# The context stream's modulation products move from VectorE to GpSimd and ScalarE in a hybrid-backbone inference step

## The chip, the core and the metric

The kernel runs on one core of a Trainium2 chip. The metric is the device time of one launch in microseconds: 1493.95 us as the median of two runs (1492.44 and 1495.47). Engines are named as in the profile: PE is TensorE (PEld its weight loads), DVE VectorE, ACT ScalarE, POOL GpSimd, SP SyncE, which here issues all DMAs. Each engine carries out its instructions in the order in which they stand in its queue; a semaphore wait at the head holds up what is behind it.

## What is computed

One inference step of a two-layer backbone on 512 latent and 128 context tokens of 1024 features. Each layer has a mixer (attention and a spatial gating in layer 0, a short gated convolution in layer 1) and a squared-ReLU MLP with 4096 hidden features. Shift, scale and gate of each come from a modulation of the two conditioning vectors, one for the latent tokens and one for the context tokens:

```python
def adaln(cvec, w_mod, b_mod):
    m = jax.nn.silu(cvec) @ w_mod + b_mod
    return [t[:, None, :] for t in jnp.split(m, 6, axis=-1)]

sh_p, sc_p, ga_p, shf_p, scf_p, gaf_p = adaln(c_ctx[None, :], w_mod, b_mod)
sh_s, sc_s, ga_s, shf_s, scf_s, gaf_s = adaln(c, w_mod, b_mod)
hs = xs * (1.0 + sc_s) + sh_s
xs = layer_norm(ALPHA * xs + ga_s * out_s, g_mix, bt_mix)
fs = sq_relu_mlp(xs * (1.0 + scf_s) + shf_s, w_ff1, w_ff2)
xs = layer_norm(ALPHA * xs + gaf_s * fs, g_ff, bt_ff)
```

## The kernel before

Everything lies feature by token: a tile has 128 features on the partitions and 640 tokens on the free axis, in two halves of 320. A float32 product is three passes of the array over operands that are split into a high and a low part. ScalarE makes the high part (line 66 for weights, 241 for a block's input `hn`, 990 for hidden features `hid`), VectorE the low part (67, 242, 992).

The weights are a stream of 188 strips of 1024x128 (`strip`, `prepare`). A strip's float32 copy is loaded into `raw`, one of four buffers, and split into one of seven `w` tiles. A strip's product with one half is 24 matmuls into one PSUM bank, of which six are used in turn. Strips 28 to 35 are the first eight up strips of layer 0's MLP, 36 to 43 its first eight down strips; three more such groups of 16 follow. The first six up strips are gone through half by half, since the norm of the second half is still being formed then; the others strip by strip.

Most of the modulation is a product on TensorE. Seven sections are not: the MLP gate of layer 0 and all six of layer 1. `mod_products` forms them "in the background" while the MLP of layer 0 runs. A section has eight steps, one for 128 features. A step loads 128 rows of the transposed modulation weights into a buffer of the same four `raw` (line 175) and forms, for both streams, the sum over 1024 columns of the weights times the conditioning row `srows` (line 178: one VectorE instruction with two inputs, whose accumulator goes to `modT`). The instruction's other output is not used. `mods` sets the rates: the first section four steps for each strip that is fetched (two strips, 34 and 35), the other six sections one step for each strip.

A scheduler sets the order of each engine's queue from the program's order and its own estimate of the times, and gives out the four `raw` buffers. An instruction of a new kind can move its neighbours.

What the prediction also speaks of: line 240 forms a block's input from the normed residual on ScalarE; line 967 scales the residual there (16 passes, not urgent); lines 989 to 992 turn an up strip's PSUM into `hid` (relu and square on ScalarE, then two VectorE passes, the first with one input in PSUM); line 1038 is a GpSimd memset.

Of the kernel before, what the change touches and what calls it, by code (L numbers as in the profile page):

```python
"""One inference step of the hybrid backbone on one core.

Everything on the chip is kept feature-major ([feature on partitions, token on the free axis]),
512 latent tokens then 128 context tokens, so that products chain without transposes, the adaLN
terms are per-partition scalars and the depthwise convolution slides along the free axis.

Float32 products: each operand is split exactly into hi + lo of 12 significant bits (float32r), and
hi*hi + hi*lo + lo*hi are three passes of the array that accumulate in float32 in PSUM.
"""
# [16 lines left out]
P = 128  # L26
D = 1024
# [15 lines left out]
AHEAD = 36  # products of the out projection before the spatial gating, which they then alternate with  # L43
WARM = (10, 18, 12)
# The attention's pieces in the order in which they are issued. By two blocks of queries: a, b the
# softmax of each, V the values; by head: C, X the same for the context, N the norm's scales, M the
# norm; F half a strip of the projections.
# [5 lines left out]
def build(ctx, tc, io):  # L53
# [9 lines left out]
    # ---------------------------------------------------------------- helpers  # L63
    def split(hl, src):
        """hl[:, 0] = hi, hl[:, 1] = lo of src (a float32 tile in SBUF)."""
        S.copy(out=hl[:, 0], in_=src)  # L66
        V.tensor_tensor(out=hl[:, 1], in0=src, in1=hl[:, 0].bitcast(F32), op=ALU.subtract)  # L67
# [3 lines left out]
    def mm3(ps, lhs, rhs, first, last):  # L71
        """ps += lhs.T @ rhs; lhs(i), rhs(i) give part i (0 hi, 1 lo)."""
        for n, (i, j) in enumerate(PASSES):
            nc.tensor.matmul(ps, lhs(i), rhs(j), start=first and n == 0, stop=last and n == 2)  # L74

    # ------------------------------------------------- the stream of weights
# [21 lines left out]
    def strip(ahead=True, behind=None):  # L98
        """The next strip; loads those ahead, and a round of the background, behind the instruction given."""
# [8 lines left out]
    # -------------------------------------------------------------- constants  # L108
# [10 lines left out]
    def start_load(out, in_):  # L119
        """The loads that the start needs, in this order."""  # L120
# [13 lines left out]
    # ------------------------------------------------------------------ adaLN  # L134
# [5 lines left out]
    # [stream, section, tile]; sections: shift, scale + 1, gate, twice  # L140
# [9 lines left out]
    def mod_section(layer, sec, ps, rows):  # L150
        """A section of a layer's modulation for both streams: KT steps and a last one."""
# [19 lines left out]
    def mod_products(layer, sec, rows):  # L171
        """A section of a layer's modulation on VectorE, from the transposed weights: KT steps."""
        for f in range(KT):
            raw = raw_tile()
            nc.sync.dma_start(out=raw, in_=io["wmodT"][6 * layer + sec - 5, f])
            for i in range(2):
                out = raw if i == 1 else tp.tile([P, D], mybir.dt.bfloat16, name="unused", tag="acc", bufs=1)
                V.scalar_tensor_tensor(out=out, in0=raw, scalar=1.0, in1=rows[:, i], op0=ALU.mult, op1=ALU.mult,  # L178
                                       accum_out=modT[layer][:, i, sec, f:f + 1])
# [14 lines left out]
    def behind(gen, rate):  # L194
        """Run rate steps of gen with every strip that is fetched."""
        background.append([gen, rate])
# [20 lines left out]
    def mod_products_start(raws, ps):  # L217
        """A feature tile of layer 0's first shift and scale: four partial sums, for both streams."""
# [5 lines left out]
    def mod_finish_start(f, ps, rows):  # L224
        """Their sum, features on partitions."""
# [8 lines left out]
    # The input of a block: x * (1 + scale) + shift, split.  # L234
    def modulate(hl, x, sc, sh, segs, tmp_pool, c0):
        """hl[:, :, cols] from x (its columns start at c0); sc(i), sh(i): [P, 1] by stream."""
# [10 lines left out]
    # =================================================== phase 1: mixer of layer 0  # L247
# [15 lines left out]
    # The start: q and k of two heads, tile by tile as the modulation's weights arrive.  # L263
# [39 lines left out]
    with tc.manual_schedule(engines={mybir.EngineType.PE}):  # L303
        start_ps[3, 0] = mmp.tile([P, HALF], F32, name="mm")

        def keep_warm(n):
            """Products that nobody reads, while there are no others: the array's clock falls when it idles."""
# [41 lines left out]
    def proj_halves(w):  # L349
        """One 128-feature strip over all tokens: the two halves' PSUM tiles, in turn."""  # L350
# [14 lines left out]
    def rotary(kind, h, f):  # L365
        """The rotary on the latent columns, split."""
# [18 lines left out]
    def token_major(consume, tile_, between=None):  # L385
        """[128 tokens, 256 features] for the five token tiles, twice; strips: k quadruples."""
# [24 lines left out]
    def softmax_pair(q, k, qc, kc, nkeys):  # L411
        """(p1 - lam p2) * 2^-E for 128 queries (columns qc) over keys kc..kc+nkeys."""
# [34 lines left out]
    def values(h, pair, es):  # L447
        """The head's values for two blocks of queries."""
# [20 lines left out]
    def context_values(h, e):  # L469
        """The same for the context's queries, which attend to the context's keys alone."""  # L470
# [10 lines left out]
    def attention_scales(h):  # L481
        """RMS norm over the head's 128 features: each token's -2 / sqrt(mean square + EPS)."""
# [30 lines left out]
    def g_consume(t, block, ps):  # L513
        """Layer norm within each group, per token."""
# [38 lines left out]
    # lambda, and a power of two that keeps the attention's output in range  # L553
# [55 lines left out]
    def gates(tag, width):  # L609
        """Two of u's strips, kept in float32."""  # L610
# [7 lines left out]
    def fillers():  # L618
        """Products that run while a softmax does."""
# [601 lines left out]
```

## Time and profile before

| | |
|---|---|
| median of the runs | 1493.95 us (1492.44, 1495.47) |
| span of the profiled execution | 1490.6 us |
| PE busy | 1477.9 us (99%) |
| DVE busy | 894.6 us (60%) |
| ACT busy | 558.2 us (37%) |
| POOL busy | 2.2 us |
| DMA | 161.85 MB, mean 109 GB/s |

The span runs from the first to the last instruction of the profiled execution; that execution's own time is not listed beside it, so the runs' median stands for it. The busy time of an engine is the time in which at least one of its instructions ran; its idle time is put down to what released it. TensorE's granted clock is at its upper level, 2.4 GHz, in each stretch shown below (1.00 in the profile's rows).

### The profile page before, as it was taken

Reading aid. Unit: us, or ns where it says so; the run is one execution under the profiler, and the core shown is the slowest. Engines: PE = TensorE matmul, PEld = TensorE weight load, DVE = VectorE, ACT = ScalarE, POOL = GpSimd, SP = SyncE. Lnnn points to the kernel's source line nnn. Section 1 sums busy time; section 2 is a strip of 40 time slices with the busy share of each in tenths; the row PEclk is TensorE's granted clock in tenths of the full one; section 3 lists DMA queues with packets and bytes.
Section 4 is the critical chain, followed back from the end, with each engine's and each line's share of the span. In section 5 each row is a group of like instructions: output and inputs, shape, how many; then the busy total and the mean of one; then the engine's idle time right before and its main releaser. Section 6 shows DMA issues by size and latency. Waiting matters only on the chain.

```text
span 1490.6 us, 24292 instructions
## 1 busy us (share of the span) xinstructions
PE 1477.9 (99%) x10126; PEld 1426.1 (96%) x10126; DVE 894.6 (60%) x1726; ACT 558.2 (37%) x1032; POOL 2.2 (0%) x11
## 2 busy tenths in 40 slices
PE   8999999999999999999999999999999999999998
PEld 7779888999999999999999999999999999999997
DVE  3656855789986596586557534449533433433456
ACT  3435655346613213213317522216712312312313
POOL 0000000000000000000000000000000000000000
PEclk9999999999999999999999999999999999999999
DMA  9762015322664274275211322212222222222102
GB/s 353 197 206 78 31 36 199 112 88 71 211 227 142 85 226 142 78 222 154 86 54 59 102 83 71 80 35 86 86 85 73 83 71 71 85 72 71 58 1 71
DMA packets 50877, 161.85 MB, mean 109 GB/s; under 512 B 8400, under 2 KB 12112, under 8 KB 50640
## 3 DMA queue, kind: packets, MB, share of 16 engines
q1 hardware_dynamic: 50768, 160.31, 33.9%
q8 instruction: 79, 1.29, 0.4%
q14 instruction: 30, 0.25, 0.0%
HBM read 157.13 MB, written 3.15 MB: 108 GB/s over the span
## 4 chain that ended last, share of the span: by engine, by line
PE 95%; DVE 2%; DMA 1%; ACT 1%; issue 0%; SPq 0%; ACTq 0%; DVEq 0%
PE mm L74 86%; PE sc L425 2%; PE mod L157 1%; PE po L74 1%; PE mm L751 1%; DMA raw<-wmod 1%; PE pt L459 1%; PE ms L221 1%; PE mm L309 0%; PE st L940 0%; DVE w L67 0%; DMA mraw<-wstart 0%; PE ss L488 0%; PE rb L504 0%; PE st L927 0%
## 5 line engine op out<-in xcount | busy, mean ns | idle before, releaser
L74 PE MATMUL mm<-hn,w 128*128 128x320 f32 x4224 | 624.8, 310 | 0.5 <-ACT hn L241 0.5
L74 PEld LDWEIGHTS mm<-hn,w 128*128 128x128 f32 x4224 | 620.4, 188 | 2.9 <-ACT hn L241 1.7
L74 PE MATMUL mm<-hid,w 128*128 128x320 f32 x3072 | 453.4, 309 | 0.0
L74 PEld LDWEIGHTS mm<-hid,w 128*128 128x128 f32 x3072 | 451.2, 188 | 0.5
L66 ACT CAST w<-raw 128x1024 fp32r<-128x1024 f32 x188 | 196.6, 1047 | 368.6 <-PE mm L74 283.5
L67 DVE TENSOR_TENSOR w<-raw,w 128x1024 fp32r<-128x1024 f32 x188 | 229.4, 1222 | 172.2 <-ACT w L66 170.9
L677 DVE SCALAR_TENSOR_TENSOR xa<-mm,modT,xa 128x128 f32<-128x128 f32 (+2 forms) x264 | 108.0, 435 | 152.5 <-PE mm L74 152.4
L989 ACT ACTIVATE relu<-mm 128x320 f32<-128x320 f32 x128 | 55.7, 436 | 236.3 <-PE mm L74 236.3
L74 PE MATMUL mm<-hin,w 128*128 128x320 f32 x576 | 97.7, 315 | 0.3 <-DVE w L67 0.2
L991 DVE TENSOR_TENSOR relu<-relu,mm 128x320 f32<-128x320 f32 x128 | 61.5, 483 | 54.9 <-ACT hid L990 54.9
L74 PEld LDWEIGHTS mm<-hin,w 128*128 128x128 f32 x576 | 85.1, 188 | 6.1 <-issue 4.3
L178 DVE SCALAR_TENSOR_TENSOR unused<-raw,srows 128x1024 bf16<-128x1024 f32 x56 | 68.4, 1221 | 33.2 <-DMA raw<-wmodT 33.1
L74 PEld LDWEIGHTS mm<-w,hin 128*128 128x128 f32 x480 | 59.4, 190 | 16.7 <-issue 15.2
L178 DVE SCALAR_TENSOR_TENSOR raw<-raw,srows 128x1024 f32<-128x1024 f32 x56 | 68.2, 1219 | 0.5
L74 PE MATMUL mm<-w,hin 128*128 128x256 f32 x480 | 65.6, 288 | 0.4 <-DVE w L67 0.4
L992 DVE TENSOR_TENSOR hid<-relu,hid 128x320 fp32r<-128x320 f32 x128 | 62.5, 491 | 3.2
L990 ACT ACTIVATE hid<-relu 128x320 fp32r<-128x320 f32 x128 | 60.2, 472 | 2.0
L74 PE MATMUL mm<-mx,w 128*128 128x320 f32 x384 | 57.5, 310 | 0.0
L74 PEld LDWEIGHTS mm<-mx,w 128*128 128x128 f32 x384 | 56.5, 188 | 0.5 <-DVE mx L67 0.2
L74 PE MATMUL mm<-mix,w 128*128 128x320 f32 x288 | 43.2, 311 | 0.0
L74 PEld LDWEIGHTS mm<-mix,w 128*128 128x128 f32 x288 | 42.5, 188 | 0.3
L240 ACT ACTIVATE hf<-xa,np 128x192 f32<-128x192 f32 (+1 forms) x72 | 36.8, 560 | 4.5 <-DVE xa L944 4.2
(218 smaller groups left out, 937.0 us busy)
## 6 DMA issues: line engine op xcount, KB each, us to landing
raw<-wall SPq DMA_DIRECT2D x188, 512.0 KB, 3.6
raw<-wmodT SPq DMA_DIRECT2D x56, 512.0 KB, 3.7
raw<-wmod SPq DMA_DIRECT2D x24, 512.0 KB, 5.2
mraw<-wstart SPq DMA_DIRECT2D x16, 512.0 KB, 10.6
x<-xT SPq DMA_DIRECT2D x4, 640.0 KB, 10.0
xa<-xT SPq DMA_DIRECT2D x8, 320.0 KB, 4.5
yT<-xa SPq DMA_DIRECT2D x8, 320.0 KB, 2.3
srows<-silu_rows SPq DMA_DIRECT2D x1, 1024.0 KB
```

Of the source, the lines that this page charges most:

```text
L66: S.copy(out=hl[:, 0], in_=src)
L67: V.tensor_tensor(out=hl[:, 1], in0=src, in1=hl[:, 0].bitcast(F32), op=ALU.subtract)
L74: nc.tensor.matmul(ps, lhs(i), rhs(j), start=first and n == 0, stop=last and n == 2)
L157: nc.tensor.matmul(ps[32 * j:32 * j + 32, :], cs[:, k, :], raw[:, b * 512:(b + 1) * 512], start=k < 2, stop=k >= KT - 2)
L178: V.scalar_tensor_tensor(out=out, in0=raw, scalar=1.0, in1=rows[:, i], op0=ALU.mult, op1=ALU.mult, accum_out=modT[layer][:, i, sec, f:f + 1])
L240: S.activation(out=hf[:, a - lo:b - lo], in_=x[:, a - c0:b - c0], func=AF.Identity, scale=sc(i), bias=sh(i))
L425: nc.tensor.matmul(scs[i][:, b, 0:n], q[r, x, qc:qc + P], k[r, y, kc + b * n:kc + (b + 1) * n], start=m == 0, stop=m == 2)
L677: V.scalar_tensor_tensor(out=xa[:, m, a:b], in0=ps[:, a - COLS[half][0]:b - COLS[half][0]], scalar=gt(i), in1=xa[:, m, a:b], op0=ALU.mult, ...
L989: S.activation(out=r, in_=ps, func=AF.Relu)
L990: evac.append(S.activation(out=hid[m][:, 0, c0:c1], in_=r, func=AF.Square))
L991: V.tensor_tensor(out=r, in0=r, in1=ps, op=ALU.mult)
L992: lows[0] = V.tensor_tensor(out=hid[m][:, 1, c0:c1], in0=r, in1=hid[m][:, 0, c0:c1].bitcast(F32), op=ALU.subtract)
```

## The change

In a step the latent stream's product stays on VectorE. The context stream's is made of two instructions: GpSimd multiplies the weights with the context row in place (line 180), and ScalarE passes the product through an identity with an accumulator, which goes to `modT` (line 181). The `raw` buffer is free once ScalarE has read it, since GpSimd writes it in place. The comments are taken out as well, so that lines from 180 on have numbers two higher.

```diff
-    def mod_products(layer, sec, rows):
-        """A section of a layer's modulation on VectorE, from the transposed weights: KT steps."""
+    def mod_products(layer, sec, rows):
         for f in range(KT):
             raw = raw_tile()
             nc.sync.dma_start(out=raw, in_=io["wmodT"][6 * layer + sec - 5, f])
-            for i in range(2):
-                out = raw if i == 1 else tp.tile([P, D], mybir.dt.bfloat16, name="unused", tag="acc", bufs=1)
-                V.scalar_tensor_tensor(out=out, in0=raw, scalar=1.0, in1=rows[:, i], op0=ALU.mult, op1=ALU.mult,
-                                       accum_out=modT[layer][:, i, sec, f:f + 1])
+            unused = tp.tile([P, D], mybir.dt.bfloat16, name="unused", tag="acc", bufs=1)
+            V.scalar_tensor_tensor(out=unused, in0=raw, scalar=1.0, in1=rows[:, 0], op0=ALU.mult, op1=ALU.mult,
+                                   accum_out=modT[layer][:, 0, sec, f:f + 1])
+            G.tensor_tensor(out=raw, in0=raw, in1=rows[:, 1], op=ALU.mult)
+            S.activation(out=raw, in_=raw, func=AF.Identity, accum_out=modT[layer][:, 1, sec, f:f + 1])
             yield
```

The order of the loads on SP is the same. TensorE's order differs at one place, the second half's first products: there the scheduler puts the matmuls of several strips in the order in which it expects `hn0` to `hn7`; the first matmul that reads `hn7` is the 62nd of this half before and the 67th now.

ScalarE's queue at that place, before (names: `hf` is a tile of the modulated input, `hn4` to `hn7` the tiles of the block's input, their numbers those of the program):

```order
L241 CAST hn4_3382<-hf_3905 128x320
L240 ACTIVATE hf_3910<-xa_2584,np00_3369 128x192
L240 ACTIVATE hf_3910<-xa_2584,np00_3369 128x128
L240 ACTIVATE hf_3916<-xa_2584,np00_3369 128x192
L241 CAST hn5_3383<-hf_3910 128x320
L240 ACTIVATE hf_3916<-xa_2584,np00_3369 128x128
L241 CAST hn6_3384<-hf_3916 128x320
```

and now:

```order
L243 CAST hn4_3382<-hf_3905 128x320
L242 ACTIVATE hf_3910<-xa_2584,np00_3369 128x128
L181 ACTIVATE raw_4332,modT0_85<-raw_4332 128x1024
L243 CAST hn5_3383<-hf_3910 128x320
L242 ACTIVATE hf_3916<-xa_2584,np00_3369 128x192
L242 ACTIVATE hf_3916<-xa_2584,np00_3369 128x128
```

The sum of the first step stands ahead of the cast of `hn5`, and two passes that stood ahead of it stand elsewhere.

ScalarE's queue around the last up strip, whose hidden tile is `hid7`, before (`xa` is the residual, `w` and `raw` a weight strip's):

```order
L990 ACTIVATE hid6_4352<-relu_4408 128x320
L967 ACTIVATE xa_2584<-xa_2584,np00_3369 128x320 x4
L989 ACTIVATE relu_4464<-mm_4439 128x320
L66 CAST w_4517<-raw_4515 128x1024
L990 ACTIVATE hid7_4438<-relu_4464 128x320
```

and now:

```order
L181 ACTIVATE raw_4422,modT0_85<-raw_4422 128x1024
L181 ACTIVATE raw_4428,modT0_85<-raw_4428 128x1024
L991 ACTIVATE relu_4412<-mm_4387 128x320
L181 ACTIVATE raw_4434,modT0_85<-raw_4434 128x1024
L992 ACTIVATE hid6_4356<-relu_4412 128x320
L181 ACTIVATE raw_4440,modT0_85<-raw_4440 128x1024
L969 ACTIVATE xa_2584<-xa_2584,np00_3369 128x320
L991 ACTIVATE relu_4472<-mm_4447 128x320
L969 ACTIVATE xa_2584<-xa_2584,np00_3369 128x320
L992 ACTIVATE hid7_4446<-relu_4472 128x320
```

The sums of steps 4 to 7 stand ahead of `hid7`. Of the 16 passes over the residual, all stood ahead of `hid7`'s relu; now seven stand ahead of `hid7`'s square and nine behind it, as do the casts of strips 39 and 40, of which one or both stood ahead.

GpSimd's queue now has, between the memsets that were there before, an instruction that waits for nothing and the 56 multiplies:

```order
L799 MEMSET minus_mean 128x128
L180 ISA
L180 TENSOR_TENSOR raw<-raw,srows 128x1024 x56
L1040 MEMSET zb_8436 128x643
L1040 MEMSET zb_8437 128x643
```

Before, the three memsets followed each other.

## Rows read from the trace of the kernel before

**Rows 1.** The page's chain that ended last: share of the span by engine.
```profile
PE 95%; DVE 2%; DMA 1%; ACT 1%; issue 0%; SPq 0%; ACTq 0%; DVEq 0%
```

**Rows 2.** Windows: stretch and length, busy us (instructions) of PE, PEld, DVE, ACT, POOL.
```profile
361.00:400.00 39.00, 38.87 (x264) 38.75 (x265) 36.94 (x68) 31.32 (x65) 0.00 (x0) 1.00 0.50 152
400.00:510.00 110.00, 110.00 (x752) 110.00 (x751) 78.47 (x137) 29.78 (x48) 0.00 (x0) 1.00 0.51 162
510.00:742.00 232.00, 232.00 (x1584) 232.00 (x1583) 166.38 (x304) 61.92 (x100) 0.84 (x2) 1.00 0.49 150
```

**Rows 3.** Lines of 362 to 742: count | busy us, mean ns | idle before.
```profile
L178 DVE SCALAR_TENSOR_TENSOR unused<-raw,srows 128x1024 bf16<-128x1024 f32 x56 | 68.4, 1221 | 33.2 <-DMA raw<-wmodT 33.1
...
L178 DVE SCALAR_TENSOR_TENSOR raw<-raw,srows 128x1024 f32<-128x1024 f32 x56 | 68.2, 1219 | 0.5
```

**Rows 4.** Timeline of 361 to 371 by engine: start us, length us, instruction, count.
```profile
361.13 12.12 PE L74 MATMUL mm<-hn,w 128*128 128x320 f32 x80 [0.52 <-ACT hn L241]
...
362.65 1.22 DVE L178 SCALAR_TENSOR_TENSOR unused<-raw,srows 128x1024 bf16<-128x1024 f32 x1
...
366.11 1.37 ACT L240 ACTIVATE hf<-xa,np 128x192 f32<-128x192 f32 x3
...
369.59 0.46 ACT L241 CAST hn<-hf 128x320 fp32r<-128x320 f32 x1
```

**Rows 5.** Timeline of 394 to 454: casts and one low part of weight strips.
```profile
394.26 1.05 ACT L66 CAST w<-raw 128x1024 fp32r<-128x1024 f32 x1 [0.24 <-DMA raw<-wall]
...
399.12 1.22 DVE L67 TENSOR_TENSOR w<-raw,w 128x1024 fp32r<-128x1024 f32 x1
...
446.03 1.05 ACT L66 CAST w<-raw 128x1024 fp32r<-128x1024 f32 x1 [5.99 <-PE mm L74]
453.07 1.06 ACT L66 CAST w<-raw 128x1024 fp32r<-128x1024 f32 x1 [5.99 <-PE mm L74]
```

**Rows 6.** Lines of the whole span by form, ScalarE.
```profile
L66 ACT CAST w<-raw 128x1024 fp32r<-128x1024 f32 x188 | 196.6, 1047 | 368.6 <-PE mm L74 283.5 <-DMA raw<-wall 54.9 <-DVE unused L178 19.2
...
L431 ACT ACTIVATION_READ_ACCUMULATOR e<-sc,st 128x1 f32 x16 | 3.1, 196 | 0.0
```

**Rows 7.** Lines of the whole span, GpSimd.
```profile
L1038 POOL MEMSET zb<- 128x643 f32 x2 | 1.2, 637 | 509.8 <-DVE raw L178 509.8
...
L128 POOL MEMSET mean_h<- 128x128 f32 x1 | 0.2, 204 | 0.3 <-POOLq L1217 0.3
```

**Rows 8.** Timeline of 395 to 401 by engine: hid7's two halves and the first down strip.
```profile
396.55 3.68 PE L74 MATMUL mm<-hid,w 128*128 128x320 f32 x24
...
398.21 0.47 ACT L990 ACTIVATE hid<-relu 128x320 fp32r<-128x320 f32 x1
...
398.01 0.49 DVE L992 TENSOR_TENSOR hid<-relu,hid 128x320 fp32r<-128x320 f32 x1
...
400.25 0.48 DVE L992 TENSOR_TENSOR hid<-relu,hid 128x320 fp32r<-128x320 f32 x1
```

**Rows 9.** Lines of 361 to 400.
```profile
L178 DVE SCALAR_TENSOR_TENSOR raw<-raw,srows 128x1024 f32<-128x1024 f32 x8 | 9.8, 1219 | 0.0
L178 DVE SCALAR_TENSOR_TENSOR unused<-raw,srows 128x1024 bf16<-128x1024 f32 x8 | 9.7, 1219 | 0.0
...
L67 DVE TENSOR_TENSOR w<-raw,w 128x1024 fp32r<-128x1024 f32 x5 | 6.0, 1220 | 0.7 <-ACT w L66 0.7
L992 DVE TENSOR_TENSOR hid<-relu,hid 128x320 fp32r<-128x320 f32 x11 | 5.3, 486 | 0.0
L991 DVE TENSOR_TENSOR relu<-relu,mm 128x320 f32<-128x320 f32 x11 | 5.2, 483 | 0.2 <-ACT hid L990 0.2
L242 DVE TENSOR_TENSOR hn<-hf,hn 128x320 fp32r<-128x320 f32 x8 | 3.9, 489 | 1.1 <-ACT hn L241 1.1
...
L967 ACT ACTIVATE xa<-xa,np 128x320 f32<-128x320 f32 x16 | 9.2, 644 | 0.0
```

**Rows 10.** Lines of 0 to 394.2, ScalarE: the casts before that at 394.26.
```profile
L66 ACT CAST w<-raw 128x1024 fp32r<-128x1024 f32 x39 | 40.7, 1048 | 23.9 <-PE mm L751 10.0 <-PE mm L74 8.2 <-DMA raw<-wall 4.8
```

## The prediction

> **What bounds the kernel now.** I read the chain of work that ended last first: TensorE holds 95% of it [rows 1]. Then the busy time by stretch [rows 2]: TensorE is busy for 38.87 of 39.00 us in 361 to 400, and all the time from 400 to 742, which is where the changed section products run. The lines of 362 to 742 show all 56 + 56 products of line 178 there, on VectorE [rows 3]. So TensorE is the bound in the whole stretch. What VectorE does there lies under it, and the change can gain almost nothing: 0.5 us of idle time of TensorE before one matmul at 361.13 [rows 4]. The question is only whether the new chain (VectorE, then GpSimd, then ScalarE) makes something late for which TensorE waits.
>
> TensorE takes a weight strip in 7.04 us here (casts follow its products at 446.03 and 453.07) [rows 5], 48 matmuls, so 0.147 us each. The profiled execution has a span of 1490.6 us; the runs have a median of 1493.95, so 3.4 us lie around the span. I add the change to the span and carry the 3.4 over.
>
> **What goes, comes and moves.** There are 56 steps: 8 at four per strip (gate of the feed-forward, 361 to 400), then 48 at one per strip.
>
> Gone from VectorE: 56 products at 1.219 us, 68 us in all [rows 3].
>
> New on ScalarE: 56 sums over 128x1024. The rows nearest are the cast of 128x1024, 1.047 us, and the accumulator read of the softmax, 0.196 us [rows 6]: 1.25 us each, 70 us in all.
>
> New on GpSimd: 56 multiplies of 128x1024 float32. No row has one. A memset costs 0.204 us at 128 columns and 0.637 at 643 [rows 7], which is 0.84 ns a column and 0.1 us fixed. One such stream makes 0.96 us at 1024 columns, the lower bound; two inputs and one output one behind the other make 2.7, the upper. I take 2.2: two inputs surely cost more than memset's none, and the output may overlap. (The Trainium skill, GPSIMD Engine Reference, section 3.1, gives 4497 ns for 2048 float32 columns; an estimate from it is 2.25 us for 1024, and the sum would be the same.)
>
> Work at one step per strip first, since most steps are there. A strip lasts 7.04 us. GpSimd has 2.2 us of work in it, ScalarE 4.2 (cast, sum, four passes over 320 columns at 0.47 [rows 8]), VectorE 4.4 (1.22 twice, four passes at 0.49 [rows 9]). All fit even with waits. In time a raw buffer is held longer, by the multiply, the sum and their place behind other work, about 4 us; four buffers serve two loads a strip. The strip cast at 394.26 is number 39 (39 casts lie before it, counted from 0) [rows 10] and its low part is there at 400.34 [rows 5]. It is the fourth of the down strips 36 to 43. TensorE starts strip 36 at 396.55 [rows 8], so it wants 39 at 396.55 + 3 x 7.04 = 417.7. That is a lead of 17.4 us and the smallest one. Eight multiplies and sums that stretch the loads ahead of it by 8 to 10 us still leave it 7. Cost at one step per strip: nothing; the cover is this lead, and without it each later strip costs its lateness.
>
> That leaves 361 to 400, where two hand-overs have no lead.
>
> First, the second half of the normed input. TensorE is behind the casts of hn by nothing: from 361.13 it runs without a gap [rows 4], and by the order its 62nd matmul is the first that reads hn7, so 361.13 + 61 x 0.147 = 370.1; that cast ends at 369.59 + 0.46 = 370.05. The change puts the sum of step 0 on ScalarE ahead of hn5's cast. It can start when the one pass that is left ahead of it is done, 366.11 + 1.37 / 3 = 366.6, if the multiply is done: VectorE's product of the step ends at 363.87, so GpSimd ends at 363.9 + 2.2 = 366.1, in time. Two passes move behind hn5's cast, which then ends at 366.6 + 1.25 + 0.45 = 368.3, and with them hn7's at about 370.9, 0.8 later than before. The matmul order has moved as well: hn7 is first read by the 67th matmul, at 370.8. Cost here: 0 to 0.5 us.
>
> Second, hid7, the last tile before the down strips. Its first half gets its low part at 398.01 to 398.50; TensorE wants it in the 23rd matmul after 396.55, at 399.8. So 1.3 us are to spare; the second half (done 400.73, wanted 403.3) has 2.6 [rows 8]. In the new order the sums of steps 4 to 7 stand on ScalarE ahead of the relu of hid7. Load of ScalarE in 361 to 400: 31.3 us [rows 2], plus 8 x 1.25, less nine residual passes at 0.575 (9.2 / 16) [rows 9] and two casts at 1.05 that now stand behind hid7: 34.0 us. That fits into 38.5 if ScalarE waits less than 4 us for GpSimd. VectorE had 36.9 us and loses 9.8: 27.1. So with GpSimd and VectorE side by side both hand-overs hold to within a fraction: +0.5 us.
>
> They may not run side by side. Nearly all that VectorE does in this stretch reads two operands in SBUF, as the multiply does: the remaining products 9.7 us, the weights' low parts 6.0, hid's low parts 5.3, and hn's 3.9 make 24.9 us; only the relu products (5.2 us) read one of theirs in PSUM [rows 9]. No row shows GpSimd reading while VectorE runs: before, GpSimd does nothing in 361 to 510 [rows 2]. Lower bound, no hindrance: +0.5. Upper bound, one at a time: 24.9 + 8 x 2.2 = 42.5 us have to go through 39.0, so hid7 is 3.5 us late, 2.2 after the 1.3 to spare, and by my estimate 2 us more, since each multiply waits for its product and each sum for its multiply (the work of one step, 2.2 + 1.25 us, stands behind the last): about +4. With multiplies of 2.7 us the load is 46.5, and it is +8. I take +4, the upper end at the likely price: VectorE has hardly an idle us in the stretch, 36.9 of 39, so any hindrance shows.
>
> (The Trainium skill, SBUF — State Buffer, section "Who interferes with whom", says that a VectorE instruction with two SBUF inputs and a GpSimd instruction that reads SBUF take turns, each whole. By that rule the sum is +4, and without it +0.5. No row here shows it yet.)
>
> Sum: 1490.6 + 4 = 1494.6 of span, 1498 us with the 3.4 around it.
>
> **Rivals.**
> No hindrance: VectorE and GpSimd run side by side, both hand-overs hold. For it: 34.0 of 38.5 us on ScalarE. Against: no slack on hn at all. 1494.5.
>
> Late first multiply: a first GpSimd instruction of a new kind may cost something that memsets do not show, and it stands ahead of hn5's cast through the sum. The order has an ISA instruction of GpSimd before it, with no wait, so it can run as soon as GpSimd's memsets ahead of it are done, long before 362. If the first multiply still took three times my upper bound, 8.1 us and not 2.2, hn5 is 6 us late and TensorE with it: 1500 without hindrance, 1504 with. (The Trainium skill, GPSIMD Engine Reference, section 2.1, has about 6 us for the first call of freshly loaded code, which would give the same times; no run here shows it.)
>
> The other side, slower by over 2%: GpSimd becomes the bound at one step per strip. Its place is the raw buffers: a weight's load waits for the sum of a step, which waits for the multiply. It decides from 7.04 us a multiply. For 30 us, the lead of 17 us has to be used up too, so (30 + 17) / 48 = 1.0 us over 7.04: 8 us a multiply, three times my upper bound. It gives 1524 and more.
>
> VectorE's relief pays: 68 us are gone, but all that TensorE could win back in 361 to 742 is the 0.5 us ahead of 361.13. 1493.5 at best.
>
> **How the numbers follow.** Chances: forecast 0.50 (its own range 1495 to 1505), no hindrance 0.36, late first multiply 0.09, GpSimd as the bound 0.04, relief 0.01. The range leaves out the GpSimd bound and the far end of the forecast with dear multiplies; at its low end it takes in no hindrance less the 1.5 us by which the two runs lie from their median: 1492 to 1506. About 2% (30 us) is what a measurement of this kernel can tell from no change. No case gains that much, only GpSimd as the bound loses it: faster 0.01, same 0.95, slower 0.04.
>
> **What would show it.** GpSimd's multiplies at 2.0 to 2.7 us. Line 178 with 56 instead of 112 products, and some of VectorE's two-operand rows longer than 1.22 and 0.49 us wherever a multiply runs: then they take turns; unchanged means they do not. TensorE's waits in 361 to 410 sum to about 4 us, for hid at line 74 first, for hn second, and to nothing in 410 to 742. ScalarE's waits for GpSimd before its sums are a few us a step at four per strip. Wrong would be: waits of TensorE for weights after 417 (the lead did not hold), a multiply over 5 us, or waits for hn5 of 5 us and more (a late first multiply).

## The result: 1.24% slower, and the profile after

The changed kernel takes 1512.6 us (1510.19 to 1515.0) against 1493.95: a ratio of 1.0124, 95% interval 1.0108 to 1.0141, 18.6 us more. The forecast was 1498, its range 1492 to 1506. That it would be slower, and by less than 2%, was right; the size was over four times too small (4 us), and the time lies 6.6 us above the range.

The windows of the changed kernel, which answer to [rows 2] (stretch and length; busy us and instructions of PE, PEld, DVE, ACT, POOL; granted clock, DMA share, GB/s):

```profile
361.00:400.00 39.00, 37.45 (x253) 36.80 (x252) 34.20 (x45) 27.52 (x60) 12.56 (x5) 1.00 0.32 108
400.00:510.00 110.00, 99.56 (x655) 97.76 (x654) 79.16 (x98) 47.45 (x80) 46.59 (x18) 0.95 0.46 154
510.00:742.00 232.00, 230.92 (x1567) 229.50 (x1565) 172.55 (x231) 93.92 (x165) 90.32 (x33) 1.00 0.45 148
```

TensorE was busy all through these stretches before. Now it idles 1.6, 10.4 and 1.1 us, most of it in the first tens of us behind 400, and its granted clock is down to 0.95 in the middle one. VectorE lost 68.2 us of products [rows 3] and yet is busy 285.9 us here against 281.8 before (36.94 + 78.47 + 166.38 [rows 2]). The windows end at the same time and not at the same work, for the changed kernel is some 22 us behind at 742. Over the whole launch, where the work is the same, VectorE is busy 914.1 us, and it was 894.6 before: 19.5 us more with 68.2 us of products less, so the rest of its instructions became some 88 us longer.

```profile
PE 1488.1 (98%) x10126; PEld 1433.1 (95%) x10126; DVE 914.1 (60%) x1614; ACT 614.8 (41%) x1144; POOL 154.1 (10%) x67
```

Where the time went shows in the lines of 362 to 765, by form (count | busy us, mean ns | idle before):

```profile
L180 POOL TENSOR_TENSOR raw<-raw,srows 128x1024 f32<-128x1024 f32 x56 | 151.9, 2715 | 377.0 <-DVE unused L178 352.0 <-DMA raw<-wall 14.6 <-ACT raw L181 10.4
L67 DVE TENSOR_TENSOR w<-raw,w 128x1024 fp32r<-128x1024 f32 x56 | 110.3, 1976 | 14.6 <-ACT w L66 14.6
L178 DVE SCALAR_TENSOR_TENSOR unused<-raw,srows 128x1024 bf16<-128x1024 f32 x56 | 74.8, 1335 | 46.7 <-DMA raw<-wmodT 46.6
L181 ACT ACTIVATE raw<-raw 128x1024 f32<-128x1024 f32 x56 | 59.4, 1061 | 196.9 <-POOL raw L180 196.9
L994 DVE TENSOR_TENSOR hid<-relu,hid 128x320 fp32r<-128x320 f32 x60 | 47.1, 786 | 1.8
L993 DVE TENSOR_TENSOR relu<-relu,mm 128x320 f32<-128x320 f32 x60 | 28.8, 482 | 27.2 <-ACT hid L992 27.1
L146 DVE SCALAR_TENSOR_TENSOR modT<-modT,bmod 128x8 f32<-128x8 f32 x4 | 6.3, 1578 | 0.7 <-ACT raw L181 0.7
```

Every VectorE form with both inputs in SBUF is longer than in [rows 9]: the weights' low parts 1.98 us instead of 1.22, hid's low parts 0.79 instead of 0.49. The relu products, which read one input from PSUM, take what they took, 0.48. The last row is the plainest: a pass over 128x8, 0.16 us in the kernel before, takes 1.58 in the mean of four, nearly all of it kept out by GpSimd (the one at 534.25 ends at 536.44, the multiply beside it at 536.41). ScalarE waited 196.9 us for GpSimd ahead of its sums, 3.5 us a step.

How far TensorE fell behind, and where, shows in the starts of its stretches. Timeline of PE in the changed kernel (start, length, instruction, count, idle before and what ended it):

```profile
364.79 4.78 PE L74 MATMUL mm<-hn,w 128*128 128x320 f32 x30 [0.52 <-ACT hn L243]
370.61 31.07 PE L74 MATMUL mm<-hn,w 128*128 128x320 f32 x210 [1.03 <-DVE hn L244]
401.51 2.95 PE L74 MATMUL mm<-hid,w 128*128 128x320 f32 x19
408.06 0.90 PE L74 MATMUL mm<-hid,w 128*128 128x320 f32 x2 [3.60 <-DVE hid L994]
413.22 0.63 PE L74 MATMUL mm<-hid,w 128*128 128x320 f32 x1 [4.26 <-ACT hid L992]
414.27 11.02 PE L74 MATMUL mm<-hid,w 128*128 128x320 f32 x62 [0.41 <-DVE hid L994]
...
469.12 24.80 PE L74 MATMUL mm<-hn,w 128*128 128x320 f32 x168
...
528.98 56.48 PE L74 MATMUL mm<-hid,w 128*128 128x320 f32 x384
...
756.64 36.68 PE L74 MATMUL mm<-hid,w 128*128 128x320 f32 x249
```

The same rows of the kernel before start at 361.13 [rows 4], 396.55 [rows 8], and then:

```profile
452.87 47.39 PE L74 MATMUL mm<-hn,w 128*128 128x320 f32 x322
...
509.19 56.48 PE L74 MATMUL mm<-hid,w 128*128 128x320 f32 x384
...
734.47 36.68 PE L74 MATMUL mm<-hid,w 128*128 128x320 f32 x249
```

So the lag is 3.66, 4.96, 16.25, 19.79 and 22.17 us. The first 3.66 are there before any changed step (its early part ran at a granted clock of 0.97 in 0 to 100); the other 18.51 are the change: **1.3 at hn**, **11.3 at the first down strip**, **5.9 in the up strips behind it**. The up strips' part differs between executions of the same kernel: in e11 below, the changed kernel again, it is 3.7. In the 11.3 are 8.27 us of waits (3.60 + 4.26 + 0.41). Most of the other 3.0 are slow matmuls behind them, by the clock:

```profile
410.00:415.00 5.00, 1.36 (x4) 1.02 (x5) 1.54 (x3) 4.75 (x10) 0.22 (x1) 0.50 0.64 206
415.00:420.00 5.00, 5.00 (x27) 5.00 (x27) 3.02 (x8) 5.00 (x10) 0.95 (x1) 0.70 0.00 0
420.00:425.00 5.00, 5.00 (x37) 5.00 (x36) 5.00 (x5) 2.74 (x4) 1.46 (x1) 1.00 0.29 61
```

Behind the waits TensorE was granted 0.50 (1.2 GHz, the lower level), and in 415 to 420 it did 27 matmuls where a full stretch has 36 or 37. The 62 matmuls from 414.27 took 11.02 us instead of 62 x 0.147 = 9.1; the rest of the 3.0 lies on the three ahead of them and on the restarts behind the waits. A stop alone, at a granted clock of 1.00 in the up strips, costs 0.2 to 0.5 us more than its recorded wait, so not all of the 3.0 is the clock. Of the 5.9 us in the up strips 3.4 are recorded waits for relu products, at seven places; the rest lies around these stops.

What made hid late stands on three engines. Timeline of the changed kernel, 397 to 413, DVE, then POOL, then ACT:

```profile
397.41 3.43 DVE L178 SCALAR_TENSOR_TENSOR unused<-raw,srows 128x1024 bf16<-128x1024 f32 x1
400.88 1.23 DVE L178 SCALAR_TENSOR_TENSOR unused<-raw,srows 128x1024 bf16<-128x1024 f32 x1
402.43 3.02 DVE L178 SCALAR_TENSOR_TENSOR unused<-raw,srows 128x1024 bf16<-128x1024 f32 x1
405.39 2.62 DVE L994 TENSOR_TENSOR hid<-relu,hid 128x320 fp32r<-128x320 f32 x1
...
397.21 2.55 POOL L180 TENSOR_TENSOR raw<-raw,srows 128x1024 f32<-128x1024 f32 x1 [2.76 <-DVE unused L178]
400.98 9.24 POOL L180 TENSOR_TENSOR raw<-raw,srows 128x1024 f32<-128x1024 f32 x3 [1.22 <-ACT raw L181]
...
399.79 1.06 ACT L181 ACTIVATE raw<-raw 128x1024 f32<-128x1024 f32 x1 [1.28 <-POOL raw L180]
...
404.40 1.06 ACT L181 ACTIVATE raw<-raw 128x1024 f32<-128x1024 f32 x1 [3.46 <-POOL raw L180]
...
407.69 1.06 ACT L181 ACTIVATE raw<-raw 128x1024 f32<-128x1024 f32 x1 [1.81 <-POOL raw L180]
...
410.25 1.06 ACT L181 ACTIVATE raw<-raw 128x1024 f32<-128x1024 f32 x1 [1.06 <-POOL raw L180]
...
411.85 0.41 ACT L991 ACTIVATE relu<-mm 128x320 f32<-128x320 f32 x1
```

The product at 397.41 takes 3.43 us: the multiply runs from 397.21 to 399.76, and the product ends 1.1 us behind it, nearly its own length (1.22). VectorE waits until GpSimd is done, then runs. It goes on in turns, and hid6's low part of the first half (405.39) ends at 408.0: the wait of 3.60 us. On ScalarE the relu of hid7's first half stands behind four sums, each of which waits for its multiply; it runs at 411.85, though its matmuls were done half a strip before 401.51, at 398.0. That is the wait of 4.26 us.

(The Trainium skill, SBUF — State Buffer, section "Who interferes with whom", has this rule: a VectorE instruction with two SBUF inputs contends with a GpSimd instruction that reads SBUF, one with at most one SBUF input, outside its 2-port modes, doesn't. The trace agrees on both: low parts of 1.98 against 1.22, relu products of 0.482 against 0.483 [rows 9].)

### The profile page after: what moved, and what is told of

Same layout as the page of the kernel before. It is cut to its first block, busy times and chain, and to the rows that moved or that the text cites. A ratio compares the mean times of both kernels' runs of the same rounds, so it can differ in the third digit from the quotient of the medians.

```text
span 1513.2 us, 24451 instructions
## 1 busy us (share of the span) xinstructions
PE 1488.1 (98%) x10126; PEld 1433.1 (95%) x10126; DVE 914.1 (60%) x1614; ACT 614.8 (41%) x1144; POOL 154.1 (10%) x67
## 4 chain that ended last, share of the span: by engine, by line
PE 73%; DMA 7%; DVE 7%; POOL 4%; ACT 4%; issue 3%; SPq 0%; POOLq 0%; ACTq 0%; DVEq 0%
PE mm L74 64%; DMA raw<-wmodT 5%; POOL raw L180 4%; DVE w L67 2%; DVE unused L178 2%; ACT raw L181 2%; PE sc L427 2%; PE mod L157 1%; PE po L74 1%; PE mm L753 1%; DMA raw<-wall 1%; DMA raw<-wmod 1%; PE mm L311 1%; PE pt L461 1%; PE ms L223 1%
## 5 line engine op out<-in xcount | busy, mean ns | idle before, releaser
L67 DVE TENSOR_TENSOR w<-raw,w 128x1024 fp32r<-128x1024 f32 x188 | 271.4, 1446 | 145.4 <-ACT w L66 144.1
L180 POOL TENSOR_TENSOR raw<-raw,srows 128x1024 f32<-128x1024 f32 x56 | 151.9, 2715 | 377.0 <-DVE unused L178 352.0
L181 ACT ACTIVATE raw<-raw 128x1024 f32<-128x1024 f32 x56 | 59.4, 1061 | 196.9 <-POOL raw L180 196.9
L178 DVE SCALAR_TENSOR_TENSOR unused<-raw,srows 128x1024 bf16<-128x1024 f32 x56 | 74.8, 1335 | 46.7 <-DMA raw<-wmodT 46.6
L994 DVE TENSOR_TENSOR hid<-relu,hid 128x320 fp32r<-128x320 f32 x128 | 80.2, 629 | 3.7
```

What stands on the lines that cost most here:

```text
L178: V.scalar_tensor_tensor(out=unused, in0=raw, scalar=1.0, in1=rows[:, 0], op0=ALU.mult, op1=ALU.mult, accum_out=modT[layer][:, 0, sec, f:f ...
L180: G.tensor_tensor(out=raw, in0=raw, in1=rows[:, 1], op=ALU.mult)
L181: S.activation(out=raw, in_=raw, func=AF.Identity, accum_out=modT[layer][:, 1, sec, f:f + 1])
L994: lows[0] = V.tensor_tensor(out=hid[m][:, 1, c0:c1], in0=r, in1=hid[m][:, 0, c0:c1].bitcast(F32), op=ALU.subtract)
```

## The experiments

All ratios are to the kernel before, on the same chip; 0.1% is 1.5 us. Differences in us are worked out from the ratios; most intervals are some 2 us wide to either side.

**e1: no multiply.**
```diff
-            G.tensor_tensor(out=raw, in0=raw, in1=rows[:, 1], op=ALU.mult)
             S.activation(out=raw, in_=raw, func=AF.Identity, accum_out=modT[layer][:, 1, sec, f:f + 1])
```


> The changed kernel without GpSimd's multiply: ScalarE sums the raw weights right behind VectorE's product, so the context half of these sections is wrong, and the 56 sums stay. Theory 1 (VectorE and GpSimd take turns at SBUF, and ScalarE's queue stands still behind the late multiply): both causes are gone; the time is back at 1492 to 1497 us, VectorE's two-operand rows are 1.22 and 0.49 us, TensorE waits under 2 us in 361 to 742. Rival 2 (ScalarE's 70 us of sums alone make hid and the relu products late): 1505 us or more, with TensorE's waits at hid and relu as in the changed kernel (8.3 and 3.4 us).


Measured: 1493.28 us, 1.0007 (0.9996 to 1.0018). TensorE's only wait is the 0.5 us at hn that was there before. All 56 sums are still on ScalarE: its 70 us (1.25 each) cost nothing. Rival 2 is out.

**e3: memsets in place of the multiply.**
```diff
-            G.tensor_tensor(out=raw, in0=raw, in1=rows[:, 1], op=ALU.mult)
+            for n in (D, D, D // 2):
+                G.memset(raw[:, 0:n], 0.0)
```


> The changed kernel with GpSimd's multiply replaced by three memsets into the same buffer (1024, 1024 and 512 columns; by the memsets of the kernel before 0.96 + 0.96 + 0.53 = 2.45 us, as long as the free multiply of 2.4), so GpSimd writes but reads nothing, and the context half is wrong. The chain VectorE, GpSimd, ScalarE and its waits stay. Theory 1 (it is the turns between two-operand VectorE instructions and a reading GpSimd that cost): VectorE's rows are back at 1.22 and 0.49 us, the memsets take 2.45 us a step, time 1493 to 1499 us. Rival 3 (the length of the chain alone, ScalarE waiting for GpSimd ahead of the relu, costs it): 1506 us or more. Rival 4 (any GpSimd access to SBUF holds VectorE): rows as long as in the changed kernel and 1506 us or more.


Measured: 1492.79 us, 1.0004 (0.9996 to 1.0013). Lines of 362 to 765 of e3:

```profile
L181 POOL MEMSET raw<- 128x1024 f32 x112 | 106.9, 958 | 373.1 <-DVE unused L178 352.1 <-DMA raw<-wall 8.9 <-ACT relu L992 4.3
L67 DVE TENSOR_TENSOR w<-raw,w 128x1024 fp32r<-128x1024 f32 x58 | 70.7, 1221 | 39.4 <-ACT w L66 39.4
L182 ACT ACTIVATE raw<-raw 128x1024 f32<-128x1024 f32 x56 | 59.3, 1059 | 112.6 <-POOL raw L181 112.4
L995 DVE TENSOR_TENSOR hid<-relu,hid 128x320 fp32r<-128x320 f32 x60 | 29.4, 491 | 1.8
```

GpSimd works 2.44 us a step (958 + 958 + 526 ns), as long as a multiply alone (2.40). The chain stays, and of ScalarE's waits for it 112.4 us of 196.9, but VectorE's rows are back at 1.22 and 0.49 and TensorE loses nothing. ScalarE's order isn't the same to the instruction, yet two sums still stand ahead of hid7's first square. What costs is that GpSimd reads SBUF; rivals 3 and 4 are out. (The Trainium skill, SBUF — State Buffer, section "Who interferes with whom", says that a GpSimd instruction that only writes SBUF doesn't contend; this run agrees.)

**e7: a one-input GpSimd instruction.**
```diff
-            G.tensor_tensor(out=raw, in0=raw, in1=rows[:, 1], op=ALU.mult)
+            G.tensor_scalar(out=raw, in0=raw, scalar1=1.0, scalar2=None, op0=ALU.mult)
```


> The changed kernel with GpSimd's two-input multiply replaced by a one-input one (times 1.0, in place in the same buffer), so the context half is wrong; chain, order and queue stay. Theory 1a (any GpSimd instruction that reads SBUF takes turns with VectorE's two-operand ones): low parts behind it as long as the multiply lasts, 1.5 us and more in the mean against 1.22; 1500 us or more if it lasts 2 us. Theory 1b (only two-input GpSimd instructions do): rows of 1.22 and 0.49 us as with the memsets, 1492 to 1496 us. It may last 0.96 (a memset) to 2.4 us (the multiply).


Measured: 1503.28 us, 1.0079 (1.0066 to 1.0091). One input is enough, as 1a says, but it holds VectorE for less: the low parts take 1.34 us in the mean, not 1.5. DVE and POOL of e7:

```profile
383.46 1.67 DVE L67 TENSOR_TENSOR w<-raw,w 128x1024 fp32r<-128x1024 f32 x1
...
382.89 2.89 POOL L180 TENSOR_SCALAR raw<-raw 128x1024 f32<-128x1024 f32 x1 [4.24 <-DVE unused L178]
```

The low part ends at 385.13, 0.65 us ahead of GpSimd's end (385.78). With the low part's own 1.22 us taken off, VectorE was kept out for about the first 1.0 us of GpSimd's instruction only, and then ran beside it. Other low parts of e7 agree: begun 0.36 and 0.84 us behind GpSimd's start (459.12 and 441.50) they take 1.76 and 1.28 us, and 0.89 us behind it (428.33) 1.23, as alone. So the instruction is longer than the multiply (2.77 us at least, against 2.40) and costs less, and 1a's "as long as the multiply lasts" is wrong for it.

**e4 and e5: one part at a time.** e4 forms only layer 1's 48 steps the new way (`if layer == 1:`, else the two VectorE products of before), e5 only the gate's eight (`if layer == 0:`).

> Only the six sections of layer 1 (48 steps at one per strip) are formed the new way; the feed-forward gate's eight steps at four per strip stay on VectorE. By the profile of the changed kernel against that of before, 12.6 us of 18.5 were lost in 361 to 430 (1.3 at hn, 11.3 at hid7) and 5.9 in 470 to 755 (waits for the relu product). Theory 1 (two separate places, each with its own lateness): 1498 to 1502 us, no wait at hid7, the relu waits stay. Rival 5 (the loss behind 470 us is only a late echo of the hid7 stall, whose loads fall in a bad place): 1492 to 1496 us and no relu waits.

> The other half of e4: only the eight steps of the feed-forward gate, at four per strip in 361 to 400, are formed the new way; the 48 steps of layer 1 stay on VectorE. e4 alone cost 5 us (1.0034). Theory 1 (two places, each by itself): the rest of the 18.6 us is here, +12 to +15 us, 1505 to 1508; TensorE waits 1 to 2 us for hn and 7 to 9 us for hid7, and its granted clock falls to 0.5 in one stretch behind that wait. Rival 5 (the two parts make each other worse, since layer 1's first loads come while the gate is late): +3 to +8 us.


Measured: e4 1496.47 us, 1.0034 (1.0021 to 1.0047), +5.1 us; e5 1506.29 us, 1.009 (1.0077 to 1.0104), +13.4 us. The sum is 18.5 us, the whole change within the intervals. e5 waits 1.0 us more for hn and 8.7 for hid, and none behind 430; e4 waits, beside the 0.5 us at hn that was there before, only for relu products. Two places, each by itself; rival 5 is out in both. The size of e4's part is loose: its interval is 3.1 to 7.0 us, its median lies below the 1498 expected, and its profiled execution lost 2.3 us between the first down strip and 738.

**e6: the sums of layer 1 later on ScalarE.** e4, with each sum issued one strip later behind the last square.
```diff
-            S.activation(out=raw, in_=raw, func=AF.Identity, accum_out=modT[layer][:, 1, sec, f:f + 1])
+            late, due = due, (raw, f)
+            total(late)
...
+        def total(step):
+            if step is not None:
+                with tc.issue_after(evac[-1].ins):
+                    S.activation(out=step[0], in_=step[0], func=AF.Identity, accum_out=modT[layer][:, 1, sec, step[1]:step[1] + 1])
```


> e4 (only layer 1 the new way) with another order: the sum of a step is issued one strip later, behind both squares of the strip before, so that no relu stands behind a sum that still waits for GpSimd. The multiplies and the turns with VectorE stay. Theory 1 (the loss in layer 1 is ScalarE's queue: relu and square behind a sum that waits 4 to 6 us): TensorE's waits for relu go from 1.1 us to 0.3 or less and the time from 1.0034 to at most 1.001 of the kernel before. Rival 6 (the lengthened rows of VectorE alone make the relu products late): 1.003 or more, waits for relu as before. Rival 7 (raw buffers that are held longer make the weights late): waits for weights, 1.005 or more.


Measured: 1492.52 us, 1.0001 (0.9992 to 1.001). TensorE waits for nothing but the 0.5 us at hn that was there before. What the order does is best seen beside the changed kernel, at a step of the up strips. First the changed kernel (DVE, POOL, ACT, PE):

```profile
493.51 1.22 DVE L67 TENSOR_TENSOR w<-raw,w 128x1024 fp32r<-128x1024 f32 x1
...
493.73 3.26 POOL L180 TENSOR_TENSOR raw<-raw,srows 128x1024 f32<-128x1024 f32 x1 [6.21 <-DVE unused L178]
...
497.02 1.06 ACT L181 ACTIVATE raw<-raw 128x1024 f32<-128x1024 f32 x1 [5.86 <-POOL raw L180]
...
498.08 0.42 ACT L991 ACTIVATE relu<-mm 128x320 f32<-128x320 f32 x1
...
499.57 7.30 PE L74 MATMUL mm<-hn,w 128*128 128x320 f32 x48 [0.60 <-DVE relu L993]
```

Here GpSimd is the one that is kept out, by the low part, so its multiply takes 3.26; the sum waits for it, the relu stands behind the sum, and TensorE for the relu product that frees its PSUM tile. Now e6 (DVE, POOL, ACT):

```profile
475.10 2.10 DVE L1008 TENSOR_TENSOR hid<-relu,hid 128x320 fp32r<-128x320 f32 x1
...
474.44 2.41 POOL L187 TENSOR_TENSOR raw<-raw,srows 128x1024 f32<-128x1024 f32 x1 [6.53 <-DVE unused L185]
...
474.45 1.04 ACT L177 ACTIVATE raw<-raw 128x1024 f32<-128x1024 f32 x1
```

The sum runs without a wait, beside the next step's multiply. hid's low part still loses 1.6 us to the turn (they take 0.87 us in the mean of 300 to 765 of e6), and nobody waits for it. So in layer 1 the whole loss reaches TensorE through the order on ScalarE, and VectorE's longer rows by themselves are free there; rivals 6 and 7 are out.

**e2: no sum.**
```diff
             G.tensor_tensor(out=raw, in0=raw, in1=rows[:, 1], op=ALU.mult)
-            S.activation(out=raw, in_=raw, func=AF.Identity, accum_out=modT[layer][:, 1, sec, f:f + 1])
```


> The changed kernel without ScalarE's sum: GpSimd multiplies, nobody sums, so the context half of these sections is left out (the modulation buffer is zeroed at the start instead). Theory 1a (most of the loss is ScalarE's queue, which stands still behind a sum that waits for GpSimd): VectorE's rows stay long (low parts near 2.0 us, hid's low parts near 0.8), but the time is 1494 to 1501 us. Theory 1b (VectorE's lengthened rows alone make hid7 late): 1505 us or more, TensorE's wait for hid 5 us or more. Rival 2 (ScalarE's load): 1492 to 1496 us with no wait at all.


Measured: 1540.91 us, 1.0321 (1.0307 to 1.0335), against every expectation: two and a half times as dear as the change with its sums. TensorE waits 19.6 us for relu products and 2.2 for `xa` behind 430, and 5.1 for hid and 3.1 for hn ahead of it. In e2 the products stand on VectorE ahead of the relu products and wait for their weights (103.4 us in 362 to 800, against 46.6 in the changed kernel), and the loads wait for the multiply. The waits of SP's queue in e2 (engine, line, waited for: us, times, longest):

```profile
SPq L86 <- POOL raw L182: 148.7, 26, 9.3
SPq L178 <- POOL raw L182: 142.1, 29, 14.1
```

Without the sums the schedule put other instructions in front of each other and gave out the raw buffers in other turns, so this run doesn't separate what it was made for. Why both loads of a strip come to wait for one multiply in it was not followed further.

**e8: the gate's steps earlier.** The sections are also started ahead of the first up strip, 28, instead of behind the first six (a second part of the edit, not shown).
```diff
-        behind(mod_products_of([(0, 5)], srows), 4)
+        behind(mod_products_of([(0, 5)], srows), 1)
```


> The changed kernel with the gate's eight steps spread over the eight up strips, one per strip from strip 28 on, instead of four each at strips 34 and 35. Same work, same instructions, other places. Theory 1 (eight multiplies of 2.4 us crowd a VectorE that is 95% busy in 361 to 400): the wait for hid7 falls from 8.3 to under 2 us, and the time to 1498 to 1503 us (the 5 us of layer 1, and up to 5 for steps that now meet the normed input hn, which has no lead). Rival 8 (the place doesn't matter, the eight steps cost what they cost): 1508 us or more.


Measured: 1516.82 us, 1.0168 (1.0153 to 1.0182): worse. The wait for hid is 0.9 us, as expected, but now four multiplies fall in 354 to 370, where the norm of the second half is formed: one wait of 9.6 us for hn and 4.0 us more. I had allowed 5 us for it. The time is in rival 8's range, but not for its reason: the place does matter. Thinner spread steps don't help when they meet a hand-over with no lead at all.

**e9: matmuls to hold the clock.** Two lots of matmuls that nobody reads, 24 in the first half and 28 in the second, ahead of hid7's products in the first down strip.
```diff
+            if warm and k == nk - 1:
+                with tc.issue_after(mm_last[0].ins):
+                    for _ in range(warm):
+                        mm_last[0] = nc.tensor.matmul(st, wv[:, 0, m0, :], srcs[0][:, 0, c0:c1], start=True, stop=True)
```


> The changed kernel with 24 and 28 matmuls more that nobody reads (0.147 us each, 3.5 and 4.1 us), in the two halves of the first down strip right ahead of hid7's products, where TensorE waited 3.6 and 4.7 us. hid7 itself comes when it comes. Theory 1 (of the 11.3 us lost there, 8.3 are waits and 3.0 the lower granted clock behind them): the clock stays at 1.00 behind 415, the waits shrink by the matmuls, and the time is 2 to 3 us below that of the changed kernel on the same chip. Rival 9 (the 3.0 us are something else, say refilling): same time as the changed kernel or more.

**e11: the changed kernel again, beside it.**


> The changed kernel itself, to stand beside the others on the same chip. By the two parts alone (1.0034 and 1.009) 1.012 to 1.013.


Measured: e11 1512.98 us, 1.0134 (1.012 to 1.0147); e9 1520.6, 1.0189 (1.0173 to 1.0205). e9 loses 7.6 us more instead of winning 3. By the two traces only 2.1 us of that are at the first down strip (70.4 us from its start to the up strips behind it, 68.3 in e11). 6.4 are in the rest up to the fourth group of down strips, where TensorE waits 4.8 us for relu products and 2.0 for `xa`, against 1.9 and nothing in e11; why was not followed. At the strip itself I had misread whom TensorE waits for: the 3.6 us are for hid6's low part, ahead of these matmuls, and both waits belong to the first half. PE in e9:

```profile
406.38 0.90 PE L75 MATMUL mm<-hid,w 128*128 128x320 f32 x2 [3.62 <-DVE hid L1001]
407.08 5.92 PE L704 MATMUL st<-hid,w 128*128 128x320 f32 x24
412.83 3.68 PE L75 MATMUL mm<-hid,w 128*128 128x320 f32 x24
416.35 4.27 PE L704 MATMUL st<-hid,w 128*128 128x320 f32 x28
```

The 24 matmuls took 5.92 us, not 3.5, since the clock had fallen in the wait ahead of them; behind them hid's own 24 ran at 3.68, full speed, where the changed kernel was still slow. That most of the missing 3.0 us are the clock fits this, but the 28 of the second half covered no wait and cost their 4.27 us, so the test gives no price of the clock.

**e10: the gate alone, without sums.** e5 without the `S.activation` line.


> e5 (only the gate the new way) without ScalarE's sums, so the gate's context half is left out (zeroed at the start); multiplies and turns with VectorE stay. e5 cost 13.1 us (1.009). Theory 1 (at hid7 both count: VectorE's turns make the first half's low part late, 3.7 us, and ScalarE's queue behind the sums the second half's relu, 4.6 us): the wait for the second half's high part is gone or under 1 us, that for the low part of the first half stays at 2 to 5 us; time +5 to +9 us, 1.0033 to 1.006. Rival 10a (the turns alone do it): 1.008 or more. Rival 10b (the queue alone): under 1.002.


Measured: 1504.99 us, 1.0088 (1.0073 to 1.0102). The waits at hid are as theory 1 has them (4.9 us for a low part, none for hid7's high part), the time is not, and lies where rival 10a puts it: waits for hn went from 1.0 to 3.0 us. That VectorE's order had moved as well is the likely reason, not a shown one, so e10 doesn't decide between theory 1 and rival 10a.

**e12: the whole change in another order.** e6's later sums, and the gate's sums of steps 4 to 7 behind both squares of hid7 (`flush` issues the sums that are still due, each behind the last square).
```diff
+                run_block(ups[6:8], "alt")
+                flush(len(due))
```


> The whole change, complete, in another order on ScalarE: in layer 1 each sum one strip later behind both squares (as in e6), and the gate's sums of steps 4 to 7 behind both squares of hid7. Two corrections to what the expectations of e9 and e10 say: in the changed kernel TensorE's 3.6 us are a wait for hid6's low part (first half), and the 4.3 and 0.4 us for hid7's, first half too. Theory 1 (VectorE's turns with GpSimd make hid6's and hid7's low parts late by 4 to 5 us, as in e10 without sums; ScalarE's queue adds the rest at hid7, and everything in layer 1): no wait for hid7's high part, a wait for a low part of 3 to 6 us, nothing behind 430; time 1.005 to 1.009 of the kernel before. Rival 11 (with the queue in order nothing is left): 1.002 or less. Rival 12 (four raw buffers held until hid7 is done make the strips' weights late): waits for weights at line 67, 1.010 or more.


Measured: 1504.36 us, 1.0079 (1.0065 to 1.0093). PE and DVE of e12:

```profile
403.05 1.17 PE L74 MATMUL mm<-hid,w 128*128 128x320 f32 x3 [3.42 <-DVE hid L1011]
406.55 23.75 PE L74 MATMUL mm<-hid,w 128*128 128x320 f32 x151 [2.32 <-DVE hid L1011]
...
400.37 2.63 DVE L1011 TENSOR_TENSOR hid<-relu,hid 128x320 fp32r<-128x320 f32 x1
```

Beyond the 0.5 us at hn that was there before, no wait for ScalarE is left, and none of any kind behind 407, as theory 1 has it. What remains is 1.0 us at hn and hid6's and hid7's low parts, late by VectorE's turns: 5.7 us of waits, and 2.3 more behind them. VectorE has no gap of note from 380 to 404, so it, and not ScalarE, is what they wait for. So about 11.8 of the 18.5 us (9.7 to 13.9 by the interval) are the turns in the gate's stretch, and the other 6.7 are lost through ScalarE's order: 5.1 in layer 1 (e4 against e6), and about 1.6 at the gate (e5 against e12, intervals that overlap, so its size stays open).

## Why the prediction was too small, step by step

- **No gain from relief.** Right. TensorE was the bound, and VectorE's 68 us were under it.
- **Turns between VectorE and GpSimd.** The mechanism was right, and e3 shows it. The likeliest case was also the right one of the two. That each turn is a whole instruction holds for the multiply (128x8 passes of 1.58 us instead of 0.16), but not for e7's one-input instruction, which kept VectorE out for some 1.0 us of its 2.9; there the measurement decides.
- **The multiply.** Taken at 2.2 us with bounds 0.96 to 2.7; alone it takes 2.40 to 2.42, with its own waits 2.72 in the mean. (From the add of 2048 columns in the Trainium skill, GPSIMD Engine Reference, section 3.1, 2.25 us for 1024 was my estimate; the measured 2.40 is 7% more.) The sum was taken at 1.25: 1.06 and 0.19 for its accumulator read, 1.25.
- **hn.** 0 to 0.5 us forecast, 1.3 measured: one low part of hn was caught by the first multiply (VectorE 1.93 us instead of 0.49).
- **hid: the failed term of the sum.** I had +4, and +8 at the upper price; it was 11.3. The prediction says that the range leaves the dear multiplies out, but +8 is 1502, inside it, and even the top of 1506 is only +12 for everything. Three things were missing. First, I added up one load, VectorE's two-operand work plus the multiplies, as if it ran without gaps; but in 361 to 410 VectorE also waited 5.4 us for ScalarE (3.4 for hn's casts, 1.6 for hid's, 0.4 for a weight's). Second, I looked at hid7's low part alone; hid6's stood behind three products, two of them held, and hid7's relu behind four sums, and TensorE waited for both, one after the other. I had counted ScalarE's load (34.0 of 38.5 us) and taken its order as harmless "if ScalarE waits less than 4 us for GpSimd"; it waited 7.2 in 361 to 400 and 14.4 up to 425. Third, behind the 8.3 us of waits TensorE's granted clock was 0.50 to 0.70: most of 3.0 us more, for which the sum had no term.
- **One step per strip: priced at nothing, 5.9 us by the trace (3.7 in e11's), 5.1 by e4.** This is the step that failed outright. I looked at the lead of the weights (17 us), and it held: TensorE never waited at line 67. But the sum isn't only the end of a raw buffer; it stands in ScalarE's queue, and the relu of the up strips stands behind it: e6 takes the loss to nothing by moving the sum alone. I should have asked of the sum, too, what is queued behind it.
- **The rivals.** A late first multiply: no, the first takes 2.53 us like the others. GpSimd as the bound: no, 2.7 of 7.04 us. No hindrance: e3 shows what it would have been, 1.0004.
- **The signs named beforehand.** Multiplies of 2.0 to 2.7 us, longer two-operand rows, hid first and hn second: as said. The waits in 361 to 410 that were to sum to about 4 us are 5.2, and 9.8 with the two for hid7 that end by 414.3. "Nothing in 410 to 742" was wrong, by those two and by the waits for relu products.

## What to carry to other kernels

Work given to GpSimd is not free for VectorE: 56 multiplies that read SBUF took 68 us of products off VectorE and gave some 88 back as longer rows, so give GpSimd what only writes, or place it where VectorE reads PSUM or rests. When a chain over engines ends on an in-order queue, price the wait of its last link, not its length: ask what stands behind it, and issue it late enough that its input is ready (e6: 5 us to nothing, by order alone). Where TensorE is the bound, the best that such a change can do is no loss.

## What was not expected of the hardware

A one-input GpSimd instruction of 128x1024 float32 took 2.77 us, longer than the two-input multiply's 2.40, and, in the case shown under e7, let VectorE go on 1.9 us before its own end (1.22 + 0.65), where the multiply held it to the end. The turns go both ways: a multiply that meets VectorE's low part takes 3.26 us instead of 2.41. Each run in which TensorE waited 4.9 to 8.7 us at hid (the changed kernel, e5, e10, e11, e12) lost another 2.3 to 3.4 us there, at a granted clock that fell to 0.50 to 0.57 in one 5 us slice behind or in the waits.
